# A hybrid SSD and attention block: the scan's float32 products at three places of a projection run, and two steps that change places

## The chip, the cores and the metric

One core of a Trainium2 chip runs the whole block as one program. The metric is the device time of one execution in microseconds (us), the median of the runs shown. The engines are named as the profile names them: PE (matrix products), PEld (its weight loads), DVE, ACT, POOL, and SP, which issues the DMAs.

## The reference

A LayerNorm, then a mixer, then a convolutional FFN, each with a residual and a LayerNorm, on x of 512 tokens by 1024 channels in float32. The mixer has two branches, an SSD (Mamba-2) scan and a sparse attention, projected, gated and summed. The change is in the SSD branch alone:

```python
xbc = jax.nn.silu(_causal_dwconv(xbc, conv_w, conv_b))
xs, Bm, Cm = jnp.split(xbc, [SSD_INNER, SSD_INNER + SSD_GROUPS * SSD_STATE], axis=-1)
...
y = _ssd_scan(xs * dt[..., None], dt * A, Bm, Cm)
y = (y + xs * D_skip[:, None]).reshape(Bsz, L, SSD_INNER)
v = (y * jax.nn.silu(z)).astype(jnp.float32).reshape(Bsz, L, SSD_GROUPS, SSD_INNER // SSD_GROUPS)
v = v * lax.rsqrt(jnp.mean(v * v, -1, keepdims=True) + LN_EPS)
return (v.reshape(Bsz, L, SSD_INNER) * norm_g).astype(z.dtype)
```

The scan goes chunk by chunk: products of C and B under a decay mask, times X, for what lies inside a chunk; states of B and X carried from chunk to chunk, times C, for the rest. There are 4 groups of 4 channel tiles (128 channels each, two heads of 64).

## The kernel before

Channels lie on the partitions and 512 tokens on the free axis. A projection is eight steps; a step is three fp32r products of 128 by 128 weights with 512 tokens (weights and activations are split into a high and a low part, `whi`/`wlo` by ACT and DVE from each loaded tile `wraw`). `in_x`, `in_b`, `in_c` project a tile of X, B or C and end in `conv_silu` (two ACT instructions, four DVE instructions out of the PSUM bank `acc`); `in_z` projects a gate; `out_br(g, s)` projects group g's normalized scan result, two halves of four steps each.

The scan's own products are plain float32. For each channel tile j of group g there are: `ssd_x` (four transposes into a `tr` bank, DVE makes `xdd` and `xd` of them, SP loads the decay tile `G` and `eaB`); `ssd_s` (states: three products into bank a or b, then a chain of four DVE instructions makes `pv`); `ssd_g` and `ssd_gm` (ACT and DVE turn `G` into the masked decay); `ssd_y` (three products of `pv` with C, into a or b, DVE multiplies them into `eaB`); and `ssd_d`, for two tiles at once (eight half-width products for each tile, into banks c and a, then `v` on DVE and POOL). Each float32 product stands in the trace as two instructions, except for transposes. Besides, for each group there are `ssd_b` (four transposes of B), `ssd_cb` (C times B and the mask `cbm`), `ssd_root` (sums of squares, a square root on DVE and POOL) and `ssd_norm` (its broadcast by four transposes, then `v` to `yhi`, `ylo`).

The order of the work is written by hand. `run(projs, items)` goes through the steps of a list of projections and issues, after step k, what `items` holds for k. `pair(g, j, at, ...)` makes the items of channel tiles j and j+1. While `chain[0]` is true, each PE instruction is made to follow the one issued before it, so PE's order is the program's. The other engines' order is made by the scheduler of the tile framework, before the kernel runs; each engine takes its list in that order. There are nine runs of the scan: a first one without `pair`, then one for each two channel tiles. PSUM has eight banks: three `acc`, two `tr`, and a, b, c. After the runs come attention, the output projection and the FFN; the top-k selection for attention (`select`, L582 to L586) stands on DVE between scan work.

Of the kernel before, what the change touches and what calls it, by code (L numbers as in the profile page):

```python
# [57 lines left out]
def tok(i):  # L58
    return slice(i * P, (i + 1) * P)
# [6 lines left out]
def half_of(h):  # L66
    return slice(h * T, (h + 1) * T)
# [3 lines left out]
def block_kernel(ctx, tc, A, out):  # L71
# [16 lines left out]
    def wt(tag, shape, name, dtype=F32):  # L88
        return wk.tile(shape, dtype, name=name, tag=tag, bufs=BUFS[tag])
# [12 lines left out]
    def st(shape, name):  # L102
        return sml.tile(shape, F32, name=name, tag=name)

    def ps(tag, bufs=1):
        return ps_.tile([P, T], F32, name="p" + tag, tag=tag, bufs=bufs)

    def acc_tile():
        return ps("acc", 3)

    def tr_tile():
        return ps("tr", 2)
# [15 lines left out]
    for i in range(NT):  # L128
        t = wt("k4" if i < 2 else "g4", [P, D], "x")
# [35 lines left out]
    def rsqrt_small(src, scale, eps, n, i=0):  # L165

        v = st([P, n], f"rs_v{n}_{i}")
        nc.vector.tensor_scalar(v, src, scale, eps, OP.mult, OP.add)
        y = st([P, n], f"rs_y{n}_{i}")
        last_pow[0] = nc.gpsimd.tensor_tensor(y, v, mhalf[:, :n], OP.pow)  # L170
        return y
# [31 lines left out]
    def w_(name, s, **kw):  # L203
        return wload(A[name][s], **kw)
# [9 lines left out]
    def mm(p, a, b, start, stop):  # L214
        pe(nc.tensor.matmul(p, a, b, start=start, stop=stop).ins)  # L215
# [35 lines left out]

    def rms_root(sqs, n):

        s4 = ps("b")
        for i in range(NT):
            for j, sq in enumerate(sqs):
                mm(s4[:, i:i + 1], sq[:, tok(i)], ones[:, 0:1], start=j == 0, stop=j == len(sqs) - 1)
        return rsqrt_small(s4[:, :NT], 1.0 / n, EPS, NT)
# [8 lines left out]
    def steps(p, w, rhs, off=0):  # L267
        for k in range(len(rhs)):
            proj(p, w, rhs, off=off, part=(k, k + 1))
            if k < len(rhs) - 1:  # L270
                yield
# [46 lines left out]
    for i, t in enumerate(xt):  # L318
# [5 lines left out]
        v, y, nm = st([P, 1], f"x_v{i}"), st([P, 1], f"x_y{i}"), st([P, 1], f"x_nm{i}")  # L324
# [270 lines left out]
    def conv_silu(dst, p, c):  # L595

        y = wt("cv", [P, T], "cv")
        nc.scalar.activation(y, p, AF.Identity, bias=cwb[:, 96 + c:97 + c], scale=cwb[:, 72 + c:73 + c])
        for k in (2, 1, 0):
            d = 3 - k  # L600
            nc.vector.scalar_tensor_tensor(y[:, d:], p[:, :T - d], cwb[:, 24 * k + c:24 * k + c + 1],  # L601
                                           y[:, d:], OP.mult, OP.add)
        nc.scalar.activation(dst, y, AF.Tanh)
        nc.vector.scalar_tensor_tensor(dst, dst, 1.0, y, OP.add, OP.mult)


    def in_b(g):

        bc = wt("k4", [P, 2, T], "bc")
        sins[g] = {"BT": bc[:, 0], "CT": bc[:, 1], "xs": [], "core": [], "v": []}  # L610
        p = acc_tile()
        yield from steps(p, w_("w_xbc", 16 + g), hT)
        conv_silu(bc[:, 0], p, 16 + g)
        yield

    def in_c(g):

        p = acc_tile()
        yield from steps(p, w_("w_xbc", 20 + g), hT)
        conv_silu(sins[g]["CT"], p, 20 + g)  # L620
        yield

    def in_x(g, j):

        p = acc_tile()
        yield from steps(p, w_("w_xbc", 4 * g + j), hT)
        xj = wt("xs", [P, T], "xs")
        conv_silu(xj, p, 4 * g + j)
        sins[g]["xs"].append(xj)
        yield  # L630

    def in_z(g, j):

        p = acc_tile()
        yield from steps(p, w_("w_z", 4 * g + j), hT)
        zs = wt("m2", [P, T], "zs")
        nc.scalar.activation(zs, p, AF.Tanh, scale=0.5)
        nc.vector.scalar_tensor_tensor(zs, zs, 1.0, p, OP.add, OP.mult)
        sins[g]["z", j] = zs
        ssd_gate(g, j)  # L640
        yield

    def out_br(g, s):

        w = w_("w_br_ssd", 4 * g + s)
        for j in range(2):
            n = 2 * s + j
            p = acc_tile()
            yield from steps(p, w, sins[g]["y"], off=T * j)
            if g == 0:  # L650
                nc.scalar.activation(mssd[:, n], p, AF.Copy)
            else:
                nc.vector.tensor_tensor(mssd[:, n], mssd[:, n], p, OP.add)
            yield
# [94 lines left out]
    def ssd_d(g, js):  # L749

        s_ = sins[g]
        yds = [ps(t) for t in "ca"]
        for j, yd in zip(js, yds):
            xd, xdd, G, eaB, pv = s_["core", j]
            for c in range(NT):
                for h in range(2):
                    mm(yd[h * 64:(h + 1) * 64, tok(c)], xd[:, c, h], G[:, h, c], start=True, stop=True)
        for j, yd in zip(js, yds):
            q = 4 * g + j
            eaB = s_["core", j][3]  # L760
            v = wt("v", [P, T], "v")
            last_v[0] = nc.vector.scalar_tensor_tensor(v, s_["xs"][j], Dv[:, q:q + 1], yd, OP.mult, OP.add)  # L762
            nc.gpsimd.tensor_tensor(v[:, P:], v[:, P:], eaB[:, P:], OP.add)  # L763
            s_["v"].append(v)
            ssd_gate(g, j)

    def ssd_gate(g, j):

        s_ = sins[g]
        if len(s_["v"]) <= j or ("z", j) not in s_:  # L770
            return
        v = s_["v"][j]
        nc.gpsimd.tensor_tensor(v, v, s_["z", j], OP.mult)
        if "ssum" not in s_:
            s_["ssum"] = wt("m2", [P, T], "ssum")
            nc.scalar.activation(s_["ssum"], v, AF.Square)
        else:
            sq = wt("m2", [P, T], "sq")
            nc.scalar.activation(sq, v, AF.Square)
            nc.gpsimd.tensor_tensor(s_["ssum"], s_["ssum"], sq, OP.add)  # L780

    AT = (2, 6, 13, 18, 28, 32, 40)

    def ssd_root(g):
        sins[g]["r"] = rms_root([sins[g]["ssum"]], 4 * T)
# [49 lines left out]
    def run(projs, items):  # L835

        k = 0
        for p in projs:
            for _ in p:
                for f, *args in items.get(k, ()):  # L840
                    f(*args)
                k += 1
        assert k > max(items), (k, items)

    def pair(g, j, at, more=(), root=11, norm=20):

        items = {}
        more = [*more]
        if g and not j:
            more += [(root, ssd_root, g - 1), (norm, ssd_norm, g - 1)]  # L850
        x0, x1, s0, s1, y0, y1, d = at
        for n in range(4):
            more += [(s0 + 1 + n, ssd_g, g, j, n), (s1 + 1 + n, ssd_g, g, j + 1, n)]
        more += [(x0, ssd_x, g, j), (x1, ssd_x, g, j + 1), (s0, ssd_s, g, j, "a"), (s1, ssd_s, g, j + 1, "b"),
                 (s1 + 4, ssd_gm, g, j), (s1 + 7, ssd_gm, g, j + 1),
                 (y0, ssd_y, g, j, "a"), (y1, ssd_y, g, j + 1, "b"), (d, ssd_d, g, (j, j + 1))]
        for k, *f in more:
            items.setdefault(k, []).append(f)
        return items

    def scored(*ks):
        return [(k, next, score, None) for k in ks]

    def pin():
# [5 lines left out]
    first_items[44] = [(ssd_cb, 0)]  # L870
    run([in_b(0), in_c(0), out_ga(0), in_x(0, 0), out_ga(1), in_x(0, 1)], first_items)
    run([in_x(0, 2), in_z(0, 0), in_x(0, 3), in_z(0, 1), in_b(1)],
        pair(0, 0, (2, 12, 15, 21, 28, 31, 37), scored(*range(1, 40, 3))))
    run([in_x(1, 0), in_x(1, 1), in_z(0, 2), in_c(1), in_z(0, 3), in_x(1, 2)],
        pair(0, 2, AT, [*scored(3, 5, 7), (21, ssd_b, 1)]))
    for g in (1, 2):
        run([in_x(g, 3), in_b(g + 1), in_z(g, 0), in_z(g, 1), out_br(g - 1, 0), out_br(g - 1, 1), in_c(g + 1)],
            pair(g, 0, AT, [(1, ssd_cb, 1), (18, t5_load), (46, t5_rows)] if g == 1 else ()))
        run([in_x(g + 1, 0), in_z(g, 2), out_br(g - 1, 2), in_x(g + 1, 1), in_z(g, 3), out_br(g - 1, 3),
             in_x(g + 1, 2)], pair(g, 2, AT, [(11, ssd_b, g + 1), (21, ssd_cb, g + 1), (42, pin)]))  # L880
    run([in_x(3, 3), in_z(3, 0), in_z(3, 1), in_z(3, 2), out_br(2, 0)],
        pair(3, 0, (0, 4, 11, 16, 25, 28, 36), [(37, pin)]))
    run([out_br(2, 1), in_z(3, 3), out_br(2, 2), out_br(2, 3)],
        pair(3, 2, (0, 3, 9, 13, 21, 23, 30)))
    chain[0] = False


# [201 lines left out]
    for i in range(NT):  # L1089
        for j in range(2):  # L1090
            t = h1[i][:, half_of(j)]
# [36 lines left out]
    for k in range(KR, KW):  # L1128
        d = [wop.tile([P, D], F32R, name=f"wo{k}{j}", tag=f"wo{k}{j}") for j in range(2)]
# [7 lines left out]
    for i in range(NT):  # L1137
# [6 lines left out]
        for j in range(2):  # L1144
            t = h1[i][:, half_of(j)]
# [221 lines left out]
```

## Time and profile before

| | |
|---|---|
| median of 3 runs | 1104.15 us (1103.95 to 1104.29) |
| profiled execution, its own time | 1103.91 us |
| its span, first to last instruction | 1102.2 us |
| mean granted TensorE clock | 0.998 |
| PE busy | 1089.3 us (99% of the span) |
| DVE, ACT, POOL busy | 772.5, 479.0, 167.3 us |

The 1.7 us between the span and the execution's time lie around the instructions. Matmuls are pipelined, so a busy PE is not a PE at its peak: how far apart matmuls start says more than how long one lasts.

### The profile page before, as it was taken

The numbers are of one execution on the slowest core, as the hardware profiler recorded it, in microseconds if no ns is written. First come the engines' busy times: TensorE is split into PE (matmuls) and PEld (weight loads), VectorE is DVE, ScalarE is ACT, GpSimd is POOL, SyncE is SP. The second block draws the span as 40 slices with busy tenths as digits, with TensorE's granted clock in tenths as the row PEclk, the third lists the DMA queues.
The fourth block names the chain that finished last, engine by engine and source line by source line (L and its number), as shares of the span: only waits on it lengthen the run. The fifth ranks groups of instructions, "written<-read, shape, count | busy, mean of one in ns | idle before, by whom it ended". The sixth has DMA issues, their size and how long they took to land.

```text
span 1102.2 us, 14649 instructions
## 1 busy us (share of the span) xinstructions
PE 1089.3 (99%) x5452; PEld 901.2 (82%) x5452; DVE 772.5 (70%) x1403; ACT 479.0 (43%) x825; POOL 167.3 (15%) x183
## 2 busy tenths in 40 slices
PE   8999999999999999999999999999999999999997
PEld 7888888788788888888787878888888888888885
DVE  7667887579967999668999958466656666542227
ACT  6345565453553643355555525115444444431220
POOL 3000203202112023023333460130000000000002
PEclk9999999999999999999999999999999999999999
DMA  7442324454244242322222356403333232322232
GB/s 285 144 150 86 117 77 136 160 177 144 87 131 134 77 134 96 120 93 74 78 72 89 125 175 203 150 1 96 98 99 98 102 99 96 97 96 95 96 96 77
DMA packets 41783, 125.71 MB, mean 114 GB/s; under 512 B 4736, under 2 KB 9392, under 8 KB 41712
## 3 DMA queue, kind: packets, MB, share of 16 engines
q1 hardware_dynamic: 41712, 124.77, 34.9%
q8 instruction: 43, 0.70, 0.3%
q14 instruction: 28, 0.23, 0.1%
HBM read 118.31 MB, written 9.59 MB: 116 GB/s over the span
## 4 chain that ended last, share of the span: by engine, by line
PE 90%; DVE 7%; issue 1%; DMA 1%; ACT 1%; POOL 0%; DVEq 0%
PE pacc L215 54%; PE pc L215 6%; PE pacc L239 6%; PE pb L215 5%; PE pa L215 4%; PE ptr L239 4%; PE ptr L215 3%; PE pb L239 2%; PE pc L239 2%; PE pa L239 2%; DVE mask L585 1%; DVE wlo L189 1%; PE pa L218 1%; DVE m L584 1%; PE ptr L218 1%
## 5 line engine op out<-in xcount | busy, mean ns | idle before, releaser
L189 DVE TENSOR_TENSOR wlo<-wraw,whi 128x1024 fp32r<-128x1024 f32 x159 | 202.1, 1271 | 184.1 <-ACT whi L188 183.6
L188 ACT ACTIVATE whi<-wraw 128x1024 fp32r<-128x1024 f32 x159 | 168.2, 1058 | 237.6 <-PE pacc L215 155.6
L215 PE MATMUL pacc<-hhi,whi 128*128 128x512 f32 (+1 forms) x536 | 219.4, 409 | 0.8 <-ACT hhi L378 0.8
L215 PE MATMUL pacc<-hlo,whi 128*128 128x512 f32 (+1 forms) x536 | 210.5, 393 | 0.8 <-DVE hlo L381 0.8
L215 PE MATMUL pacc<-hhi,wlo 128*128 128x512 f32 (+1 forms) x536 | 209.0, 392 | 0.4 <-DVE wlo L189 0.3
L215 PEld LDWEIGHTS pacc<-hlo,whi 128*128 128x128 f32 (+1 forms) x536 | 100.5, 187 | 24.7 <-DVE hlo L381 2.3
L215 PEld LDWEIGHTS pacc<-hhi,whi 128*128 128x128 f32 (+1 forms) x536 | 100.9, 188 | 19.4 <-issue 1.5
L215 PEld LDWEIGHTS pacc<-hhi,wlo 128*128 128x128 f32 (+1 forms) x536 | 100.9, 188 | 18.2 <-DVE wlo L189 0.7
L215 PE MATMUL pacc<-h1hi,wlo 128*128 128x512 f32 (+1 forms) x216 | 79.0, 366 | 0.0
L215 PE MATMUL pacc<-h1hi,whi 128*128 128x512 f32 (+1 forms) x216 | 78.9, 366 | 0.0
L215 PE MATMUL pacc<-h1lo,whi 128*128 128x512 f32 (+1 forms) x216 | 78.7, 366 | 0.0
L964 POOL TENSOR_TENSOR tm<-mask,toe 128x128 f32<-128x128 f32 (+1 forms) x64 | 44.5, 699 | 159.5 <-DVE mn L975 97.2
L1251 POOL TENSOR_TENSOR rs_y<-rs_v,mhalf 128x1 f32<-128x1 f32 x4 | 4.0, 1002 | 353.8 <-DVE rs_v L1250 349.2
L601 DVE SCALAR_TENSOR_TENSOR cv<-pacc,cwb,cv 128x511 f32<-128x511 f32 (+2 forms) x72 | 53.3, 741 | 0.5
L215 PE MATMUL pacc<-ylo,whi 128*128 128x512 f32 x128 | 50.3, 393 | 1.3 <-DVE ylo L175 1.3
L215 PE MATMUL pacc<-yhi,whi 128*128 128x512 f32 x128 | 51.6, 404 | 0.0
L215 PE MATMUL pacc<-yhi,wlo 128*128 128x512 f32 x128 | 49.9, 390 | 0.0
L763 POOL TENSOR_TENSOR v<-v,eaB 128x384 f32<-128x384 f32 x16 | 17.0, 1079 | 210.2 <-DVE v L762 147.9
L978 ACT ACTIVATE l<-l,mn 128x128 f32<-128x128 f32 (+1 forms) x64 | 35.7, 558 | 30.3 <-DVE mn L975 28.9
L215 PEld LDWEIGHTS pacc<-h1hi,whi 128*128 128x128 f32 x216 | 40.8, 189 | 6.7
L215 PEld LDWEIGHTS pacc<-h1hi,wlo 128*128 128x128 f32 x216 | 40.8, 189 | 6.5
L215 PEld LDWEIGHTS pacc<-h1lo,whi 128*128 128x128 f32 x216 | 40.5, 188 | 6.5
(481 smaller groups left out, 2268.7 us busy)
## 6 DMA issues: line engine op xcount, KB each, us to landing
wraw<-in_w_up_dram SPq DMA_DIRECT2D x44, 512.0 KB, 3.5
wraw<-in_w_xbc_dram SPq DMA_DIRECT2D x24, 512.0 KB, 3.5
wraw<-in_w_down_dram SPq DMA_DIRECT2D x22, 512.0 KB, 3.5
G<-ac_d SPq DMA_DIRECT2D x16, 512.0 KB, 5.6
wraw<-in_w_z_dram SPq DMA_DIRECT2D x16, 512.0 KB, 3.5
wraw<-in_w_br_ssd_dram SPq DMA_DIRECT2D x16, 512.0 KB, 3.5
wraw<-in_w_ga_dram SPq DMA_DIRECT2D x8, 512.0 KB, 3.5
eaB<-ea_d SPq DMA_DIRECT2D x32, 128.0 KB, 5.5
```

Of the source, the lines that this page charges most:

```text
L188: nc.scalar.activation(hi[:, :cols], raw[:, :cols], AF.Copy)
L189: nc.vector.tensor_tensor(lo[:, :cols], raw[:, :cols], hi[:, :cols].bitcast(F32), OP.subtract)
L215: pe(nc.tensor.matmul(p, a, b, start=start, stop=stop).ins)
L218: pe(nc.tensor.transpose(p, a, b).ins)
L239: nc.tensor.matmul(p, x[a][:, tok(i)], w[b][h], start=first and j == 0, stop=last and j == 2)
L584: nc.vector.max(out=m8, in_=S)
L585: nc.vector.match_replace(out=S, in_to_replace=m8, in_values=S, imm_value=-3.4e38)
L601: nc.vector.scalar_tensor_tensor(y[:, d:], p[:, :T - d], cwb[:, 24 * k + c:24 * k + c + 1], y[:, d:], OP.mult, OP.add)
L763: nc.gpsimd.tensor_tensor(v[:, P:], v[:, P:], eaB[:, P:], OP.add)
L964: nc.gpsimd.tensor_tensor(tm[:, :K - f], maskt[i][:, f:], self.toe[:, 2 * P - K + f:], OP.add)
L978: nc.scalar.activation(l[:, :K], l[:, :K], AF.Exp, bias=self.mn[:, ic], scale=-1.0, accum_out=self.sm[:, ic])
L1251: nc.gpsimd.tensor_tensor(y, v, mhalf[:, :1], OP.pow)
```

## The change

`pair` takes three places in place of seven: x (both `ssd_x`), s (both `ssd_s`, behind `ssd_root` of the group before where there is one) and y (both `ssd_y` and then `ssd_d`). `ssd_root` takes bank c in place of b, and `ssd_d` takes c and a `tr` tile in place of c and a. `ssd_cb` and `ssd_b` stand where a pair's products stand already. In groups 1 and 2, `in_c(g + 1)` goes from the end of the first run into the second, and `out_br(g - 1, 2)` from the second run to the end of the first. The masked decay of the first run of groups 1 and 2 (`gm`) is issued at 26 and 29.

```diff
     def rms_root(sqs, n):
-        s4 = ps("b")
+        s4 = ps("c")
...
     def ssd_d(g, js):
         s_ = sins[g]
-        yds = [ps(t) for t in "ca"]
+        yds = [ps("c"), tr_tile()]
...
-    AT = (2, 6, 13, 18, 28, 32, 40)
+    AT = (3, 12, 38)
...
-    def pair(g, j, at, more=(), root=11, norm=20):
-
-        items = {}
-        more = [*more]
+    def pair(g, j, at, more=(), norm=None, gm=None):
+
+        x, s0, y = at
+        gm = gm or (s0 + 7, s0 + 11)
+        items = {x: [(ssd_x, g, j), (ssd_x, g, j + 1)],
+                 s0: [(ssd_s, g, j, "a"), (ssd_s, g, j + 1, "b")],
+                 y: [(ssd_y, g, j, "a"), (ssd_y, g, j + 1, "b"), (ssd_d, g, (j, j + 1))]}
         if g and not j:
-            more += [(root, ssd_root, g - 1), (norm, ssd_norm, g - 1)]
-        x0, x1, s0, s1, y0, y1, d = at
+            items[s0].insert(0, (ssd_root, g - 1))
+            more = [*more, (norm or s0 + 7, ssd_norm, g - 1)]
         for n in range(4):
-            more += [(s0 + 1 + n, ssd_g, g, j, n), (s1 + 1 + n, ssd_g, g, j + 1, n)]
-        more += [(x0, ssd_x, g, j), (x1, ssd_x, g, j + 1), (s0, ssd_s, g, j, "a"), (s1, ssd_s, g, j + 1, "b"),
-                 (s1 + 4, ssd_gm, g, j), (s1 + 7, ssd_gm, g, j + 1),
-                 (y0, ssd_y, g, j, "a"), (y1, ssd_y, g, j + 1, "b"), (d, ssd_d, g, (j, j + 1))]
-        for k, *f in more:
+            more = [*more, (s0 + 1 + n, ssd_g, g, j, n), (s0 + 6 + n, ssd_g, g, j + 1, n)]
+        for k, *f in [*more, (gm[0], ssd_gm, g, j), (gm[1], ssd_gm, g, j + 1)]:
             items.setdefault(k, []).append(f)
         return items
...
     run([in_x(0, 2), in_z(0, 0), in_x(0, 3), in_z(0, 1), in_b(1)],
-        pair(0, 0, (2, 12, 15, 21, 28, 31, 37), scored(*range(1, 40, 3))))
+        pair(0, 0, (10, 18, 36), scored(1, 4, 7, 14, 16, 20, 22, 24, 26, 28, 30, 32, 34)))
     run([in_x(1, 0), in_x(1, 1), in_z(0, 2), in_c(1), in_z(0, 3), in_x(1, 2)],
-        pair(0, 2, AT, [*scored(3, 5, 7), (21, ssd_b, 1)]))
+        pair(0, 2, AT, [*scored(0, 8, 10), (38, ssd_b, 1)]))
     for g in (1, 2):
-        run([in_x(g, 3), in_b(g + 1), in_z(g, 0), in_z(g, 1), out_br(g - 1, 0), out_br(g - 1, 1), in_c(g + 1)],
-            pair(g, 0, AT, [(1, ssd_cb, 1), (18, t5_load), (46, t5_rows)] if g == 1 else ()))
-        run([in_x(g + 1, 0), in_z(g, 2), out_br(g - 1, 2), in_x(g + 1, 1), in_z(g, 3), out_br(g - 1, 3),
-             in_x(g + 1, 2)], pair(g, 2, AT, [(11, ssd_b, g + 1), (21, ssd_cb, g + 1), (42, pin)]))
+        run([in_x(g, 3), in_b(g + 1), in_z(g, 0), in_z(g, 1), out_br(g - 1, 0), out_br(g - 1, 1), out_br(g - 1, 2)],
+            pair(g, 0, AT, gm=(26, 29), more=[(12, ssd_cb, 1), (18, t5_load), (46, t5_rows)] if g == 1 else ()))
+        run([in_x(g + 1, 0), in_z(g, 2), in_c(g + 1), in_x(g + 1, 1), in_z(g, 3), out_br(g - 1, 3),
+             in_x(g + 1, 2)], pair(g, 2, AT, [(12, ssd_b, g + 1), (38, ssd_cb, g + 1), (42, pin)]))
     run([in_x(3, 3), in_z(3, 0), in_z(3, 1), in_z(3, 2), out_br(2, 0)],
-        pair(3, 0, (0, 4, 11, 16, 25, 28, 36), [(37, pin)]))
+        pair(3, 0, (1, 10, 34), [(37, pin)]))
     run([out_br(2, 1), in_z(3, 3), out_br(2, 2), out_br(2, 3)],
-        pair(3, 2, (0, 3, 9, 13, 21, 23, 30)))
+        pair(3, 2, (1, 9, 29)))
```

## Rows read from the trace of the kernel before

**Rows 1.** The page: the chain that ended last, by engine.

```profile
PE 90%; DVE 7%; issue 1%; DMA 1%; ACT 1%; POOL 0%; DVEq 0%
```

**Rows 2.** Windows over the scan, 93 to 418 us: their sum, busy us by engine.

```profile
sum 325.00, PE 323.58 PEld 268.12 DVE 264.82 ACT 166.50 POOL 54.31; mean PE 40.45 PEld 33.51 DVE 33.10 ACT 20.81 POOL 6.79
```

**Rows 3.** The chain in order of time, an FFN projection: start, us, what.

```profile
768.16 5.44 PE pc L215 x24
```

**Rows 4.** PE's groups by shape, 93 to 418 us: count | busy, mean ns.

```profile
L215 PE MATMUL pa<-xdd,bt 128*128 128x128 f32 x48 | 6.7, 276 | 0.0
```

**Rows 5.** Timeline of PE, group 2: transposes, root and states (start us, us).

```profile
268.43 0.39 PE L215 MATMUL pacc<-hlo,whi 128*128 128x512 f32 x1
268.66 0.60 PE L218 MATMUL ptr<-ident,xs 128*128 128x128 f32 x4
...
272.33 0.39 PE L215 MATMUL pacc<-hlo,whi 128*128 128x512 f32 x1
272.56 0.95 PE L215 MATMUL pb<-ones,ssum 128*128 128x1 f32 x8
...
274.62 0.39 PE L215 MATMUL pacc<-hlo,whi 128*128 128x512 f32 x1
274.85 0.83 PE L215 MATMUL pa<-xdd,bt 128*128 128x128 f32 x6
...
278.73 0.39 PE L215 MATMUL pacc<-hlo,whi 128*128 128x512 f32 x1
```

**Rows 6.** Timeline of PE, group 3: root and states at one place.

```profile
365.10 0.39 PE L215 MATMUL pacc<-hlo,whi 128*128 128x512 f32 x1
365.33 0.95 PE L215 MATMUL pb<-ones,ssum 128*128 128x1 f32 x8
366.14 0.92 PE L215 MATMUL pa<-xdd,bt 128*128 128x128 f32 x6
...
370.11 0.39 PE L215 MATMUL pacc<-hlo,whi 128*128 128x512 f32 x1
```

**Rows 7.** Timeline of PE around one `ssd_d`.

```profile
204.42 0.39 PE L215 MATMUL pacc<-ylo,whi 128*128 128x512 f32 x1
204.74 1.09 PE L215 MATMUL pc<-G,xd 128*64 128x128 f32 x16
...
206.64 0.50 PE L215 MATMUL pacc<-yhi,whi 128*128 128x512 f32 x1
```

**Rows 8.** Waits of PE, 93 to 418 us: total, times, longest.

```profile
PE pacc L215 <- DVE ylo L175: 1.3, 2, 1.1
```

**Rows 9.** Timelines of DVE and PE at the longer of these waits.

```profile
291.41 1.21 DVE L720 TENSOR_TENSOR G<-G,cbm 128x1024 f32<-128x1024 f32 x1
...
293.20 1.28 DVE L175 TENSOR_TENSOR ylo<-v,yhi 128x512 fp32r<-128x512 f32 x2
...
293.94 0.50 PE L215 MATMUL pacc<-ylo,whi 128*128 128x512 f32 x1 [1.10 <-DVE ylo L175]
```

**Rows 10.** Timeline of POOL: the square root of group 1's `ssd_root`.

```profile
274.97 1.01 POOL L170 TENSOR_TENSOR rs_y<-rs_v,mhalf 128x4 f32<-128x4 f32 x1 [12.72 <-DVE rs_v L168]
```

**Rows 11.** The page, DMA issues: count, KB each, us to landing.

```profile
G<-ac_d SPq DMA_DIRECT2D x16, 512.0 KB, 5.6
```

**Rows 12.** Timelines of ACT, DVE and PE: group 0's second X tile.

```profile
98.00 1.06 ACT L188 ACTIVATE whi<-wraw 128x1024 fp32r<-128x1024 f32 x1 [1.57 <-PE pacc L215]
...
99.63 0.62 ACT L603 ACTIVATE xs<-cv 128x512 f32<-128x512 f32 x1
...
100.90 0.68 DVE L604 SCALAR_TENSOR_TENSOR xs<-xs,cv 128x512 f32<-128x512 f32 x1
...
101.94 0.60 PE L218 MATMUL ptr<-ident,xs 128*128 128x128 f32 x4
```

**Rows 13.** Timelines of PE and DVE: transposes of the last pair, their evictions.

```profile
391.58 0.60 PE L218 MATMUL ptr<-ident,xs 128*128 128x128 f32 x4
...
394.06 0.68 DVE L703 TENSOR_TENSOR xd<-ptr,dt 128x512 f32<-128x512 f32 x1
```

## The prediction

> **What bounds the kernel now.** I read four views. First the chain of work that ended last: 90% of it is PE and 7% DVE [rows 1], so a change gains what it takes off PE's time line, and loses what PE then waits for. Second the windows over the scan, the only part that the change touches: in 325 us PE is busy 323.6, DVE 264.8 (81%), ACT 166.5 [rows 2]. A busy PE hides small losses, so the third view is the timeline of PE, read by the distance from one start to the next. The undisturbed distance is that of an FFN projection, where 24 fp32r products take 5.44 us [rows 3]: 0.2267 us for a product, 0.68 us for a step of three. What lies above that in the scan is what can be won. Fourth are PE's waits in the scan: a single kind, for `ylo`, twice, 1.3 us in all [rows 8]. So little is to be won, and the work is to find what can be lost.
>
> **A switch between float32 and fp32r.** The number of places at which PE goes over to float32 products and back follows from the lists of items. Before: seven for each of 8 pairs, 56; one `ssd_b` for group 1; in group 1's two runs `ssd_cb`, `ssd_root`, `ssd_norm`, `t5_rows`, `ssd_b`, `ssd_cb`; in group 2's four of these; in group 3's `ssd_norm`. That is 68. After: three for each pair, 24, three `ssd_norm` and `t5_rows`, 28. So 40 switches go; no product does.
>
> What is one worth? In the timeline of group 2 [rows 5] the fp32r product ahead of the transposes starts at 268.43 and the fifteenth behind them at 272.33. Of these 3.90 us, 15 x 0.2267 = 3.40 are fp32r, so the four transposes cost 0.50. They stand (0.60 - 0.28) / 3 = 0.11 apart (one lasts 0.28, [rows 4]), 0.44 for four: 0.06 is left for the switch. The six state instructions take 278.73 - 274.62 - 3.40 = 0.71 and stand (0.83 - 0.28) / 5 = 0.11 apart, 0.66: 0.05 is left. A merged place exists: in group 3 root and states share one [rows 6], and 370.11 - 365.10 - 3.40 = 1.61 us. Apart, in group 2, the root takes 274.62 - 272.33 - 6 x 0.2267 = 0.93, and with the 0.71 that is 1.64. Merging saved 0.03, though only six products stand behind that root to show its whole price. I take 0.05, with bounds 0.03 and 0.06: 40 x 0.05 = **2.0 us gained** (1.2 to 2.4). The switch shows as a loss in the rows; the Trainium skill's TensorE: Matmul & The Clock Gate, Part 2, has PE pull weight loads ahead of running products, by which a switch should cost nothing, and by that rule this term is 0 (a rival below).
>
> **`ssd_d` behind `ssd_y`.** Its half-width products start 0.32 us after the last fp32r product, 0.09 more than the usual 0.23 [rows 7]. Behind a full-width float32 product no `ssd_d` stands in the trace. If the array needs no pause there, the 0.09 goes, 8 x 0.09 = 0.7 us gained; if the 0.32 stays, counted from the start of a product that takes 0.11, the loss beyond its pitch is 0.21, 0.12 more than before, 8 x 0.12 = 1.0 us lost. I take 0, between the two: a float32 instruction occupies 0.11 where the fp32r one occupies 0.23, so a pause measured from the end of either would be alike. The row shows a pause at the entry; the Trainium skill's TensorEngine Tiling (Array Packing), Key Properties, says why: changing the tiling mode "drains the TensorE". By this rule eight changes in and eight out stay, whatever stands ahead of them.
>
> **The waits for `ylo`.** In group 2's first run `out_br` reaches a product for which `ylo` is not ready: PE starts at 293.94, after 1.10 us of waiting. DVE did the masked decay (`ssd_gm`, 1.21 us from 291.41) ahead of the two `ylo` it needed [rows 9]. Afterwards these two instructions are issued at 26 and 29, behind `ssd_norm` at 19, which itself comes a step earlier (20 before), and the `pv` chains are done from step 12 on. That takes 2.4 us of DVE from ahead of `ylo`, more than the 1.1 that was missing. So **1.3 us gained**, with bounds 0 (DVE's order is the scheduler's and may keep the old one) and 1.3. Next late there would be the eviction of an `out_br` half, with three `acc` banks for cover: two more halves, 8 steps, 5.4 us.
>
> **The two moved steps.** `in_c` brings its 24 products, a weight load on SP, its split on ACT and DVE, two more ACT and four more DVE instructions; `out_br` its 24 products, load, split and two evictions. They trade slots, so SP still passes one 512 KB weight load for each projection, in the same queue behind the same neighbours. DVE gets the conv later; `ssd_cb` needs C at 38, and `in_c` ends at 23: 15 steps, 10.2 us, cover it. Cost 0; bound, if C is late, what DVE is behind by, 3.2 us in the worst row below. `ssd_x`'s loads on SP move too: `G` takes 5.6 us to land [rows 11], and from x to the first `ssd_g` there are 10 steps (9 in the last pair), 6.8 (6.1) us. If one came later, ACT would stand at it with the weight splits behind; the buffer is freed two steps earlier than before (`ssd_d` at 38 for 40), which is the cover. Cost 0.
>
> **Bank and root.** `ssd_norm` follows `ssd_root` by seven steps, nine before. Its square root ended at 275.98 [rows 10], some 2.6 us behind the root's last products, and seven steps are 4.8 us. Bank c and the second `tr` bank have been read many steps before their next use. Cost 0.
>
> **The first pair.** Its transposes of the second X tile ran at 101.94; the tile was ready at 100.90 + 0.68 = 101.58 [rows 12], 0.4 us early. They now come at step 10 for 12: two steps (1.36) and a score (two short products, some 0.35) earlier, about 100.2. Ready as before, the tile would hold PE for 1.4 us. But its tanh on ACT (99.63) waited behind a weight split that itself stood 1.57 us for PE, and DVE loses two evictions (1.2 us) from ahead of the conv. If the conv ends before 98.0 the tanh fits into that gap. Bounds 0 and 1.4; I take 0.2, since the gap is longer than the tanh. **0.2 us lost.**
>
> **The sum.** 2.0 + 1.3 - 0.2 = 3.1 us. The profiled execution took 1103.91 us (span 1102.2, 1.7 around it), so 1100.8; the median of the runs is 0.24 above that execution, so the forecast is 1101.0. A change of 0.2%, 2.2 us, is about what can be told from none: below 1101.9 is faster, above 1106.4 slower.
>
> **The rivals.**
> 1. DVE keeps the waits for `ylo`. For: DVE is at 81%, and its order is decided before the run. Against: `ssd_gm` now follows in program order. 1101.0 + 1.3 = 1102.3. Chance 0.15.
> 2. A switch costs nothing once the places are merged, so the change doesn't do what it says: the merged row saved just 0.03. 1101.0 + 2.0 = 1103.0. Chance 0.09.
> 3. `ssd_d`'s entry pays 0.32 behind float32 too: 1101.0 + 1.0 = 1102.0. Chance 0.10.
> 4. The second X tile holds PE in the first pair for the whole 1.4: 1101.0 + 1.2 = 1102.2. Chance 0.10.
> 5. Slower: DVE is late with `xdd`. Both tiles' transposes come at once, and both states products nine steps later (8 in two pairs), 6.1 us, for 11 and 12 steps before. In the last pair the eviction of one tile ended at 394.74, 3.2 us after its transposes began [rows 13]; with the second tile's pair behind it (1.2) that is 4.4 us, 1.7 short of 6.1. So it takes DVE another 1.7 us behind to cost anything, and 2.4 at each of eight places to cost 5.6 us: 1106.6. For: the bursts (two `eaB`, two `v`, two pairs of evictions) are twice as long. Against: PE asks for no eviction during a long float32 place. Chance 0.12, with what else makes PE wait often.
>
> The forecast itself has 0.44, with a range of its own from 1099.8 (2.4 + 1.3 + 0.7 gained off 1103.91, and the median's 0.24) to 1102.0 (1.2 + 1.3 gained, 0.4 of new waits lost).
>
> **The numbers.** The range must leave out two in ten: 1099.2 to 1105.0 takes in everything but the slower case and a little of each end; below 1099.8 only waits smaller than those that the profile names could go. Faster: 0.40 of the forecast's 0.44, half of rivals 3 and 4 (0.10), a little of 1 and 2 (0.05): 0.55. Slower: 0.12 and 0.02 from the others: 0.14. No change that can be told: 0.31.
>
> **What would show it.** In the new profile each pair has three float32 places, root and states as one of 1.6 us; the start of the scan to its end is some 3 us shorter, all later stages shifted alike. PE's waits in the scan lose the row for `ylo`. The first product of `ssd_d` shows its distance to the last `ssd_y` product: 0.11, 0.2 or 0.32. PE's waits for `xdd`, `xs`, `G` or a `tr` bank would show the rivals. I am wrong if such waits add up to over 2 us, or if DVE's order in the second runs, which now hold four convs, makes PE wait for an `acc` bank.

## The result, and the profile after

The changed kernel takes 1109.64 us, the median of 6 runs (1108.36 to 1110.97); the kernel before took 1104.09 beside it. The ratio is 1.0051, with a 95% interval from 1.0038 to 1.0064: slower by 5.5 us, where 3 us of gain were forecast. The profiled execution is the longest of the six, 1110.97 us with a span of 1109.2, 7.06 us above that of before.

The views of [rows 1], [rows 2] and [rows 8] come first: the chain by engine; windows over the scan with two of the stretches (us, busy us and count by engine, granted clock, DMA share, GB/s); PE's waits in the scan (total, times, longest).

```profile
PE 94%; DVE 3%; ACT 2%; issue 0%; DMA 0%; POOL 0%; DVEq 0%
```

```profile
165.00:207.00 42.00, 39.77 (x193) 33.20 (x192) 30.18 (x46) 22.59 (x43) 8.66 (x7) 0.96 0.39 114
...
253.00:300.00 47.00, 43.91 (x229) 36.68 (x229) 45.11 (x98) 23.32 (x44) 10.01 (x8) 0.95 0.37 103
...
sum 325.00, PE 319.18 PEld 267.19 DVE 260.56 ACT 165.44 POOL 55.99; mean PE 53.20 PEld 44.53 DVE 43.43 ACT 27.57 POOL 9.33
```

```profile
PE pacc L215 <- DVE zs L638: 5.3, 2, 3.1
PE ptr L215 <- ACT rel L512: 0.4, 1, 0.4
```

The chain looks better than before, 94% PE for 90%, which says nothing of the time. The windows say where to look: PE stands idle for 42 - 39.77 = 2.2 us and 47 - 43.91 = 3.1 us in two stretches, the first runs of groups 1 and 2, where the clock too is below 1. The waits name the cause: not `ylo` any more, but `zs`, the last DVE instruction of a gate (`in_z`). The timeline of PE in group 1 and a window behind the wait show the price:

```profile
197.17 0.39 PE L215 MATMUL pacc<-hlo,whi 128*128 128x512 f32 x1
199.79 0.78 PE L215 MATMUL pacc<-yhi,whi 128*128 128x512 f32 x1 [2.23 <-DVE zs L638]
200.37 0.63 PE L215 MATMUL pacc<-yhi,wlo 128*128 128x512 f32 x1
200.79 0.63 PE L215 MATMUL pacc<-ylo,whi 128*128 128x512 f32 x1
...
203.55 0.40 PE L215 MATMUL pacc<-yhi,whi 128*128 128x512 f32 x1
```

```profile
200.00:203.00 3.00, 3.00 (x8) 2.32 (x9) 3.00 (x5) 0.00 (x0) 0.00 (x0) 0.50 0.64 175
```

`out_br`'s first product starts 2.62 us behind the product ahead of it, 2.39 beyond its pitch. Behind the wait the products stand up to 0.43 us apart and the granted clock is 0.50, the lower of its two levels (1.2 GHz): to 203.55 nine products take 3.76 us for 2.04, another 1.7. The same places in group 2:

```profile
292.60 0.39 PE L215 MATMUL pacc<-hlo,whi 128*128 128x512 f32 x1
296.07 0.80 PE L215 MATMUL pacc<-yhi,whi 128*128 128x512 f32 x1 [3.09 <-DVE zs L638]
...
302.46 0.40 PE L215 MATMUL pacc<-yhi,whi 128*128 128x512 f32 x1
```

The wait costs 3.24 us beyond the pitch, and the 15 products up to 302.46 another 6.39 - 3.40 = 3.0. That is 10.3 us at two places.

The rest goes into the 7.06 as follows. In the first pair PE waited for a score's relu (`rel`) and lost 0.8 at two products (0.24 and 0.58 beyond the pitch); the two old waits [rows 8] are gone, 1.65 by their pitches. That makes 10.3 + 0.8 - 1.65 = 9.45, so some 2.4 us were gained elsewhere. The merged places gave 2.0 to 2.25 of them by medians (shown below); the small rest was not followed, and executions of the kernel before alone differ by 0.4.

**Why a bank is late.** Group 1 shows it best: PE gets to `out_br` at the same time as before (the product ahead starts at 197.17, 197.08 before). ACT's timeline after and, in the second fence, before:

```profile
182.80 2.14 ACT L712 ACTIVATE G<-G,acT 128x128 f32<-128x128 f32 x7
...
185.83 2.44 ACT L712 ACTIVATE G<-G,acT 128x128 f32<-128x128 f32 x8
...
190.07 0.77 ACT L598 ACTIVATE cv<-pacc,cwb 128x512 f32<-128x512 f32 x1
```

```profile
183.49 2.44 ACT L712 ACTIVATE G<-G,acT 128x128 f32<-128x128 f32 x8
...
186.78 0.77 ACT L598 ACTIVATE cv<-pacc,cwb 128x512 f32<-128x512 f32 x1
...
188.55 2.45 ACT L712 ACTIVATE G<-G,acT 128x128 f32<-128x128 f32 x8
```

Each tile's decay passes (`ssd_g`) are tied behind that tile's copy of `pv`, and so behind its states. With both states at one place ACT does both tiles' passes in one stretch, and the first pass of `in_b`'s convolution (L598), which stood between them, starts 3.3 us later, at 190.07. DVE's list, after and before:

```profile
189.41 2.72 DVE L795 SCALAR_TENSOR_TENSOR v<-v,ngh,pc 128x512 f32<-128x512 f32 x4 [2.45 <-PE pc L218]
...
194.32 0.74 DVE L601 SCALAR_TENSOR_TENSOR cv<-pacc,cwb,cv 128x511 f32<-128x511 f32 x1
194.98 1.21 DVE L720 TENSOR_TENSOR G<-G,cbm 128x1024 f32<-128x1024 f32 x1
196.11 1.89 DVE L175 TENSOR_TENSOR ylo<-v,yhi 128x512 fp32r<-128x512 f32 x3
...
199.05 0.68 DVE L638 SCALAR_TENSOR_TENSOR zs<-zs,pacc 128x512 f32<-128x512 f32 x1
199.65 0.74 DVE L601 SCALAR_TENSOR_TENSOR cv<-pacc,cwb,cv 128x510 f32<-128x510 f32 x1
```

```profile
186.92 1.22 DVE L189 TENSOR_TENSOR wlo<-wraw,whi 128x1024 fp32r<-128x1024 f32 x1 [2.43 <-ACT whi L188]
188.06 0.74 DVE L601 SCALAR_TENSOR_TENSOR cv<-pacc,cwb,cv 128x511 f32<-128x511 f32 x1
...
193.91 0.73 DVE L601 SCALAR_TENSOR_TENSOR cv<-pacc,cwb,cv 128x509 f32<-128x509 f32 x1
```

Before, DVE did the convolution's first pass at 188.06 and its third at 193.91, and a bank was free. Now it stands idle for 2.45 us just then; the convolution begins at 194.32, behind `v`, a mask and a weight split, and at 199.65 it is in its second pass. The idle time is not the difference, since DVE stood idle for 2.43 us before too; what came behind it is. ACT explains 3.3 of the 6.3 us by which DVE's first pass comes later. The rest is the order of DVE's list, which has `v`, the mask and the split first, though ACT's pass had ended at 190.84. All three `acc` banks are held, one by the convolution and two by gates, and `out_br` gets the one that `zs` frees.

### The profile page after: what moved, and what is told of

It is laid out like the page before. It is cut to its first block, busy times and chain, and to the rows that moved or that the text cites. A ratio compares the mean times of both kernels' runs of the same rounds, so it can differ in the third digit from the quotient of the medians.

```text
span 1109.2 us, 14634 instructions
## 1 busy us (share of the span) xinstructions
PE 1091.3 (98%) x5452; PEld 905.7 (82%) x5452; DVE 774.6 (70%) x1403; ACT 477.8 (43%) x825; POOL 169.5 (15%) x183
## 4 chain that ended last, share of the span: by engine, by line
PE 94%; DVE 3%; ACT 2%; issue 0%; DMA 0%; POOL 0%; DVEq 0%
PE pacc L215 57%; PE pc L215 7%; PE pacc L239 6%; PE pb L215 5%; PE pa L215 4%; PE ptr L239 4%; PE ptr L215 3%; PE pb L239 2%; PE pc L239 2%; PE pa L239 2%; ACT G L712 1%; PE pa L218 1%; PE ptr L218 1%; PE pb L218 1%; DVE wlo L189 0%
## 5 line engine op out<-in xcount | busy, mean ns | idle before, releaser
L215 PE MATMUL pacc<-hhi,whi 128*128 128x512 f32 (+1 forms) x536 | 216.1, 403 | 0.8 <-ACT hhi L378 0.8
```

## The experiments

Three theories were set against each other. T1: the merged states make ACT's burst of decay, and the convolution behind it holds up DVE and the banks (the 5.7 us of its expectations is group 2's figure, in which PE's own loss in group 1 is contained; group 1 shows 3.3). T2: what counts is DVE's two masks ahead of `zs`. T3: the two projections that change places load DVE here. Later came T4: in group 2's first run DVE itself is the engine without slack. Times are medians; the ratio is to the kernel before, run beside each (1104.02 to 1104.22); the last column is PE's waits in the scan by that view (total, times, longest; "none" where it lists none).

| kernel | us | ratio, 95% interval | PE waits for |
|---|---|---|---|
| changed | 1109.64 | 1.0051 [1.0038, 1.0064] | zs 5.3, 2, 3.1; rel 0.4, 1, 0.4 |
| 1 states apart | 1103.60 | 0.9996 [0.9987, 1.0004] | zs 2.3, 1, 2.3; ylo 0.3, 1, 0.3 |
| 2 projections back | 1110.61 | 1.0061 [1.0048, 1.0073] | zs 5.3, 2, 3.1; rel 0.4, 1, 0.4; mssd 0.4, 1, 0.4 |
| 3 masks behind zs | 1105.28 | 1.0010 [1.0001, 1.0019] | zs 1.4, 2, 0.8; ylo 0.8, 1, 0.8; rel 0.4, 1, 0.4; cv 0.2, 1, 0.2 |
| 4 decay held | 1102.82 | 0.9986 [0.9977, 0.9995] | zs 1.4, 1, 1.4; rel 0.4, 1, 0.4 |
| 5 idle filled | 1106.90 | 1.0026 [1.0015, 1.0036] | rel 0.4, 1, 0.4; zs 0.2, 1, 0.2 |
| 6 states alone merged | 1109.21 | 1.0042 [1.0029, 1.0054] | zs 4.9, 3, 2.2 |
| 7 = 1, rounds moved | 1101.30 | 0.9977 [0.9968, 0.9986] | cv 0.8, 1, 0.8; ylo 0.3, 1, 0.3 |
| 8 = 4, rounds moved | 1100.70 | 0.9970 [0.9959, 0.9982] | rel 0.4, 1, 0.4 |
| 9 before, rounds moved | 1102.74 | 0.9986 [0.9978, 0.9995] | ylo 0.5, 2, 0.2 |
| 10 changed, rounds moved | 1109.10 | 1.0042 [1.0029, 1.0054] | zs 5.1, 2, 2.9; rel 0.4, 1, 0.4 |
| 11 = 8, first pair apart | 1099.89 | 0.9961 [0.9948, 0.9975] | none |
| 12 transposes spread | 1105.83 | 1.0014 [1.0006, 1.0023] | pv 1.1, 1, 1.1; rel 0.5, 1, 0.5; ylo 0.2, 1, 0.2 |

**1. The second tile's states apart again.**

```diff
-                 s0: [(ssd_s, g, j, "a"), (ssd_s, g, j + 1, "b")],
+                 s0: [(ssd_s, g, j, "a")], s0 + 5: [(ssd_s, g, j + 1, "b")],
```

> One edit to the changed kernel: the states of a pair's second tile (ssd_s) stand five steps behind the first tile's, as they stood before the change; everything else stays merged. Theory T1 (both state places at one point let ACT do both tiles' decay in one stretch, in_b's convolution comes 5.7 us later, DVE's work piles up ahead of zs, and out_br waits for an acc bank): out_br's two waits, 2.2 and 3.1 us after the change, fall to 1 us or less each, the granted clock stays at its upper level behind them, and the time is 1101 to 1104 us, some 6 to 8 below the changed kernel's 1109.6. Eight more switches at 0.05 us give back 0.4 us of that. Theory T2 (the two masks issued together on DVE ahead of zs, whatever ACT does): here the masks' items stay at their steps, so the waits stay at 2 us or more, 1108 to 1110. Theory T3 (the two projections that change places): the waits stay, 1109 to 1110.

The one edit took back 6 us, to a time that can't be told from that of before. Group 1's wait is gone altogether, as T1 says and T2 and T3 don't; in group 2 a wait of 2.3 us is left, which T1 did not expect. Its timeline of PE:

```profile
287.65 0.39 PE L215 MATMUL pacc<-hlo,whi 128*128 128x512 f32 x1
290.34 0.50 PE L215 MATMUL pacc<-yhi,whi 128*128 128x512 f32 x1 [2.30 <-DVE zs L638]
290.67 0.39 PE L215 MATMUL pacc<-yhi,wlo 128*128 128x512 f32 x1
290.90 0.40 PE L215 MATMUL pacc<-ylo,whi 128*128 128x512 f32 x1
```

Behind this wait the products stand 0.23 us apart: the clock did not fall in this execution.

**2. The two projections back at their old places.**

```diff
-        run([in_x(g, 3), ..., out_br(g - 1, 1), out_br(g - 1, 2)],
+        run([in_x(g, 3), ..., out_br(g - 1, 1), in_c(g + 1)],
-        run([in_x(g + 1, 0), in_z(g, 2), in_c(g + 1), ...
+        run([in_x(g + 1, 0), in_z(g, 2), out_br(g - 1, 2), ...
```

> The changed kernel with in_c(g + 1) and out_br(g - 1, 2) back at their old places; the three merged places stay. T1 and T2: what stands ahead of out_br's first product is the same, both waits stay within 0.5 us of 2.2 and 3.1 us, and the time is 1108.5 to 1110.5 us. T3 (the exchange of the two projections loads DVE at this place): both waits go, 1100 to 1103 us.

The same two waits to a tenth, and one of 0.4 us more: T3 falls. The median is 1.0 us above the changed kernel's, 0.1 beyond the expected range, with executions from 1109.56 to 1112.45: no gain or loss by the exchange of the steps can be told.

**3. The masks behind the gate on DVE.** In the first run of groups 1 and 2 both `ssd_gm` are ordered behind `zs`.

```diff
+        if g in (1, 2) and j < 2:
+            tc.add_manual_dep(i.ins, sins[g]["zi", 0].name, NOSYNC, reason="order")
```

> The changed kernel, with DVE's two masks (ssd_gm, 2.4 us together) of the first run of groups 1 and 2 put behind zs, the gate's last DVE instruction; nothing else moves, ACT's burst of decay stays. T2 (the two masks make zs late): zs ends 2.4 us earlier, the waits of 2.2 and 3.1 us fall to 0 and 0.7 us, no lower clock behind them, so all 10.3 us that the two places lose come back: 1099 to 1102 us. T1 in its strict form (what is late is in_b's convolution, behind ACT's burst): zs still waits for its place behind the convolution's own DVE work, some 1 to 1.5 us of each wait stays: 1102 to 1106 us. If the masks are then late for ssd_y, PE waits there for G and this is seen as a row of its own.

`zs`'s waits fell to 0.6 and 0.8 us, between what the two theories said, and 1.0 us of new waits came behind them, for `ylo` and for the convolution (`cv`). The masks are a part of the queue ahead of `zs`; with them out of it DVE is late with the next thing. The time, 1105.28 us, lies in T1's range. ACT's burst stayed (the convolution's first pass on ACT at 189.90), and yet 4.4 us came back: the burst does its harm mostly through what stands ahead of `zs` in DVE's list.

**4. The second tile's decay held on ACT.** All products stay at the merged places; in the first run of groups 1 and 2 the second tile's decay passes come behind the convolution's first pass in ACT's list.

```diff
+            if g in (1, 2) and j == 1:
+                tc.add_manual_dep(i.ins, last_conv[0].ins.name, NOSYNC, reason="order")
```

> The changed kernel, with the second tile's four decay passes on ACT (8 instructions, some 2.5 us) of the first run of groups 1 and 2 held behind the first ACT pass of in_b's convolution; all products on PE stay at their places. T1 (ACT's burst delays in_b's convolution): the convolution's first pass starts 2.5 us earlier or more, DVE does it ahead of the masks, both waits of out_br fall to 1 us or less, the clock stays up, 1100 to 1104 us. T2 (the masks): the waits stay above 1.5 us in both groups, 1106 to 1110 us.

ACT's and DVE's timelines in group 1 (lines two to four higher than those of after):

```profile
183.29 2.15 ACT L714 ACTIVATE G<-G,acT 128x128 f32<-128x128 f32 x7
...
188.22 0.77 ACT L600 ACTIVATE cv<-pacc,cwb 128x512 f32<-128x512 f32 x1
188.88 2.44 ACT L714 ACTIVATE G<-G,acT 128x128 f32<-128x128 f32 x8
```

```profile
189.68 0.74 DVE L603 SCALAR_TENSOR_TENSOR cv<-pacc,cwb,cv 128x511 f32<-128x511 f32 x1
...
195.97 0.74 DVE L603 SCALAR_TENSOR_TENSOR cv<-pacc,cwb,cv 128x509 f32<-128x509 f32 x1
```

The convolution stands between the two tiles' passes again, 1.85 us earlier than in after (less than the 2.5 expected); DVE starts it 4.6 us earlier and is through with its third pass before 197, and `out_br` waits no more in group 1. So 6.8 us come back with not one product moved on PE, and with both masks still ahead of `zs` in DVE's list (187.40 and 194.23): the states' place on PE was not the cost, but what it released on ACT and, behind that, the order of DVE's list. Group 2 keeps 1.4 us, more than T1 said.

**5. The idle time filled.** Products that nothing reads stand ahead of the two waits.

```diff
+    def fill(n):
+        p = tr_tile()
+        for i in range(n):
+            mm(p, hT[0][0][:, :P], hT[1][0], start=i == 0, stop=i == n - 1)
...
+            more=[(31, fill, 9), ...] if g == 1 else [(31, fill, 13)]
```

> The changed kernel with products that nothing reads put into the two idle stretches: ahead of out_br's first product in the first run of group 1 nine fp32r products of 128x512 (9 x 0.227 = 2.0 us), in that of group 2 thirteen (2.9 us), into a tr bank. DVE's and ACT's lists stay, so zs comes as late as before and the wait itself stays paid (what is left of idle is 0.2 us at each place); only the idleness goes. If the lower clock behind the two waits comes from the idleness, the products behind them stay at 0.227 us a piece, and the time falls by what the lower clock cost, 1.8 and 3.4 us in the profiled execution and by the granted clock of the others somewhat less: 1104 to 1107 us, and a narrower spread of the executions. If the lower clock is something else (the products of out_br themselves, or the time of day), the pitches of 0.427 us stay and the time is 1109 to 1111.

(By the pitches shown above, the lower clock cost 1.7 and 3.0 us, not 1.8 and 3.4.)

```profile
291.25 3.11 PE L215 MATMUL ptr<-hhi 128*128 128x512 f32 x13
294.49 0.50 PE L215 MATMUL pacc<-yhi,whi 128*128 128x512 f32 x1
294.83 0.39 PE L215 MATMUL pacc<-yhi,wlo 128*128 128x512 f32 x1
295.06 0.40 PE L215 MATMUL pacc<-ylo,whi 128*128 128x512 f32 x1
```

`out_br` comes 3.24 us behind the first filling product, as late as its wait made it, and behind it the pitch is 0.23. The time falls by 2.7 us, and eight runs lie within 0.5 us (1106.76 to 1107.23) where the changed kernel's six spread over 2.6. So half of the 5.5 us lost is the clock, which falls here because PE stands idle.

**6. Only the states merged, in the kernel before,** in the first run of groups 1 and 2 alone.

```diff
-(s1, ssd_s, g, j + 1, "b"),
+(s0 if g in (1, 2) and not j else s1, ssd_s, g, j + 1, "b"),
```

> The kernel before, with one edit: in the first run of groups 1 and 2 the states of the second tile stand beside the first tile's, five steps earlier; all other places, steps and masks are those of before. T1 (this merge alone makes ACT's burst of decay): in_b's convolution on ACT starts 4 us or more later in both runs, out_br or what stands behind it waits for an acc bank 1.5 to 3.5 us in each, and the time is 1106 to 1111 us. Rival (the burst does harm only together with the other merged places or the masks' steps): at most one wait of over 1 us, 1103 to 1105.

Six products moved by five steps, in two of the runs, cost 5 us: T1. The convolution's first pass came 2.75 us later in group 1 (189.53 on ACT, for 186.78 before), less than the 4 us expected, and 4.7 us later in group 2 (284.40 for 279.70); the waits came in both, 2.25 us in group 1, 1.66 and 0.96 in group 2. The masks stand at their old steps here, so T2 is not needed for the waits.

**7 to 10. The top-k rounds.** Experiments 1 and 4 left a wait in group 2 alone, where DVE also works at the top-k rounds of the first attention mask (`select`), tied by `pin` to group 1's last result. The edit ties them to group 2's first run.

```diff
-             ...] if g == 1 else ()))
+             ...] if g == 1 else [(42, pin)]))
...
-             ..., (38, ssd_cb, g + 1), (42, pin)]))
+             ..., (38, ssd_cb, g + 1), *([(42, pin)] if g == 2 else [])]))
```

On top of experiment 1: 

> The kernel with the second tile's states apart again, and besides the top-k rounds of the first mask (22 rounds of some 0.85 us on DVE between 250 and 293 us) tied to a scan result of group 2 in place of group 1, so that they start some 48 us later. Theory T4 (in group 2's first run DVE is the engine without slack, 44.4 of 47 us, and that is why 2.3 us of wait were left there): the wait goes or falls under 0.4 us, 1100 to 1102 us, faster than the kernel before. Rival (DVE is as late for lack of the convolution's ACT pass): the wait stays over 1.5 us, 1103 to 1104. If the rounds come too late for the attention stage, the time is lost there and the row of the wait is gone all the same.

On top of experiment 4: 

> The kernel with all three places merged and the second tile's decay held behind in_b's convolution on ACT, and besides the first mask's top-k rounds moved out of group 2's first run as in the run beside it. T4: the wait of 1.4 us goes, 1100.5 to 1102 us, the fastest or the second fastest here. Rival: it stays, 1102.5 to 1103.

In the kernel before: 

> The kernel before, with the one edit that moves the first mask's top-k rounds out of group 2's first run. The wait of 1.10 us for ylo at 293.94 stands in that run, where DVE had 46.2 of 47 us; it should go, the one of 0.23 us in group 1 stay, and the later stages be unchanged: 1102.6 to 1103.4 us. If this edit alone gave most of what the kernel with held decay and moved rounds gains (1100.7), so 1101.5 or less, then the merged places would be worth next to nothing; by the switch at 0.03 to 0.05 us the merged places are worth 1.2 to 2 us of the 3.3.

In the changed kernel: 

> The changed kernel with the one edit that moves the first mask's top-k rounds out of group 2's first run; ACT's burst of decay stays. T1: group 1 has no top-k rounds, so its wait of 2.2 us stays; in group 2 DVE has slack, but the convolution's ACT pass still comes late, so a wait of 1.0 to 2.4 us is left of the 3.1; 1105.5 to 1108.5 us. Rival (DVE without slack is the whole cause in group 2): the wait there falls under 0.5 us, 1104 to 1105.5.

The window of group 2's first run, of experiment 4 and, in the second fence, of 8:

```profile
253.00:300.00 47.00, 45.55 (x244) 37.61 (x243) 44.80 (x97) 23.68 (x44) 7.93 (x8) 1.00 0.34 106
```

```profile
253.00:300.00 47.00, 46.96 (x252) 39.28 (x251) 35.86 (x56) 24.52 (x46) 8.90 (x8) 1.00 0.35 115
```

DVE goes from 44.8 to 35.9 us and PE's last wait in the run with it: T4 holds, though experiment 7 keeps 0.8 us where under 0.4 was expected. In the kernel before the same edit takes 1.45 us off, within the forecast, so moving the rounds accounts for less than half of the 3.3 us that experiment 8 gains. In the changed kernel it gives 0.5 us, less than the spread of either kernel (1107.19 to 1110.43 with the edit), and the wait stays 2.9; DVE there even stands idle for ACT:

```profile
280.25 0.69 DVE L604 SCALAR_TENSOR_TENSOR xs<-xs,cv 128x512 f32<-128x512 f32 x1 [1.71 <-ACT xs L603]
```

More slack on DVE does not help while the burst on ACT stands: the wait was more than the 1.0 to 2.4 us expected and the time, 1109.10, above its range, which speaks for T1 and against DVE's load as the whole cause. The two bind one after the other.

**11. The states of the first pair apart, on top of 8.**

```diff
-                 s0: [(ssd_s, g, j, "a"), (ssd_s, g, j + 1, "b")],
+                 s0: [(ssd_s, g, j, "a")],
...
+        items[s0 if g or j else s0 + 5] = items.get(s0 if g or j else s0 + 5, []) + [(ssd_s, g, j + 1, "b")]
```

> The fastest kernel so far (three merged places, the second tile's decay held on ACT in groups 1 and 2, the first mask's rounds moved), and in the first pair the second tile's states five steps behind the first's. In the first pair the burst of decay on ACT stood ahead of the scores' relu, two waits of PE, 0.24 and 0.59 us beyond the pitch; apart they should go, for one or two switches at 0.05: 1099.9 to 1100.4 us.

The two waits for a score's relu go, and 0.8 us with them: the same burst on ACT, in another run. This version beats both kernels, by 4.3 us and 9.75.

**12. The transposes spread.** Each `ssd_x` puts one transpose behind each of four steps.

```diff
             mm_t(tr[:, c], x_[:, tok(c)], ident)
+            if c < NT - 1 and (g or j > 1):
+                yield
```

> The kernel before, with the four transposes of a channel tile put one behind each of four steps in place of all behind one (seven of the eight pairs): 41 more places at which PE goes over to float32 and back, and not one product more. If a switch costs 0.05 us, 2.0 us lost: 1105.8 to 1106.6 us; at 0.026 (what the first product behind a place shows) 1.1 us: 1105.0 to 1105.5; if a switch costs nothing, 1104.0 to 1104.5. In the trace the first fp32r product behind a single transpose starts later than the pitch by the price.

```profile
221.36 0.40 PE L215 MATMUL pacc<-hlo,whi 128*128 128x512 f32 x1
221.60 0.27 PE L218 MATMUL ptr<-ident,xs 128*128 128x128 f32 x1
221.63 0.48 PE L215 MATMUL pacc<-hhi,whi 128*128 128x512 f32 x1
...
222.40 0.27 PE L218 MATMUL ptr<-ident,xs 128*128 128x128 f32 x1
```

The time alone would fit 0.04 us a switch, but new waits for `pv` (1.1) and a relu (0.5) are in it, and the old wait of 1.10 is out, so it can't be read as the price. The rows can: a step with one transpose takes 222.40 - 221.60 = 0.80 us, 0.12 over 0.68, of which the transpose is 0.11; 43 such steps in this trace take 0.81 on average. With three products between switches, one costs some 0.01 to 0.02 us.

## Why the prediction was wrong

**The switches: right.** The timeline of PE after, in group 2, answers to [rows 5]: both tiles' transposes, then root and both states at one place.

```profile
269.94 0.39 PE L215 MATMUL pacc<-hlo,whi 128*128 128x512 f32 x1
270.17 1.03 PE L218 MATMUL ptr<-ident,xs 128*128 128x128 f32 x8
...
274.24 0.39 PE L215 MATMUL pacc<-hlo,whi 128*128 128x512 f32 x1
...
276.96 0.39 PE L215 MATMUL pacc<-hlo,whi 128*128 128x512 f32 x1
277.19 0.95 PE L215 MATMUL pc<-ones,ssum 128*128 128x1 f32 x8
278.00 0.91 PE L215 MATMUL pa<-xdd,bt 128*128 128x128 f32 x6
278.75 0.83 PE L215 MATMUL pb<-xdd,bt 128*128 128x128 f32 x6
...
282.61 0.39 PE L215 MATMUL pacc<-hlo,whi 128*128 128x512 f32 x1
```

By the same sum as in the prediction, to the fifteenth product behind: 274.24 - 269.94 - 3.40 = 0.90 for eight transposes, for 2 x 0.50 apart, 0.10 for one switch; and 282.61 - 276.96 - 3.40 = 2.25 for 0.93 + 0.71 + 0.71, 0.10 for two. From the kernel before with moved rounds to experiment 11 the time falls 2.85 us; its two remaining waits were worth 0.8 (two pitches of 0.62 for 0.23), and 2.05 is left for 39 switches (2.25 if the 0.20 us that one product is late in experiment 11, at 290.22, are counted), 0.05 to 0.06 each. So the 2.0 us were there, and rival 2 is wrong. What the prediction drew from the Trainium skill's TensorE: Matmul & The Clock Gate, Part 2, that with weight loads pulled ahead a switch should cost nothing, is not borne out by these rows.

**`ssd_d` behind `ssd_y`: right, at 0.** In the first run of group 1 its first product stands 0.77 us behind the start of six float32 ones 0.11 apart, so 0.22 behind the last, 0.11 beyond the pitch; 0.09 before [rows 7]. Rival 3 is wrong.

```profile
206.94 0.83 PE L215 MATMUL pb<-bc,pv 128*128 128x128 f32 x6
207.71 1.09 PE L215 MATMUL pc<-G,xd 128*64 128x128 f32 x16
```

**The waits for `ylo`: the step that failed.** The prediction held that the masks, issued at 26 and 29, would go from ahead of `ylo`, and that next late would be the eviction of an `out_br` half, "with three `acc` banks for cover". The masks did not go: in group 1 DVE still does both ahead of `ylo` (the second at 194.98, `ylo` at 196.11). The waits for `ylo` vanished because PE already stood at `out_br`'s first product, for something later. And the cover wasn't there: when `out_br` begins, its three banks are held by the convolution and two gates, none of them by an `out_br` half. The prediction asked which wait goes and which instructions move on DVE; it didn't follow ACT's list, where the decay is tied to the states that the change moves, and so costed the moved states by their products alone. The text does name the outcome, PE waiting for an `acc` bank, among what would make it wrong, but lays it to the four convs of the second runs. It came in the first runs.

**The clock: no term at all.** The sum priced a wait at its own length. Here 5.6 us of waiting beyond the pitch brought another 4.7, nearly all at the lower clock, in the profiled execution; in the median it was 2.7, by what filling the idle time gave back.

**The first pair: a size not far off, another place.** 0.2 was put down, 0.8 measured, and not for the second X tile, whose transposes ran at 100.33 without a wait [rows 12], but for the scores behind ACT's burst. Rival 4 is wrong in its mechanism.

**The moved steps, the bank and the root: right, at 0** (experiment 2 for the steps; for the bank and the root, no wait of PE for them stands in the trace). Rival 5, slower because DVE is late with `xdd`: the sign came true, but no wait for `xdd` stands in the trace. Rival 1 had the reason right, DVE's list keeping the masks ahead of `ylo`, but not the wait: none for `ylo` is left. With the burst taken apart and the rounds moved the changed places run at 1099.9 to 1101.3: the forecast's 1100.8 is about the time of the changed kernel without its new waits (1110.97 - 10.3 - 0.8 = 1099.9).

## What to carry to other kernels

When an edit moves products together, list what each of them releases on the other engines, and what stood between those two pieces of work in their lists; that, and not the products, may set the price. Ask of the first wait that you remove which wait comes one instruction ahead of it, and count who holds each buffer at that moment. On a PE with almost no idle time a wait of two or three microseconds can cost nearly twice its length (here 5.6 us became 10.3), in some executions and not in others.

## What the runs showed of the hardware that was not expected

Behind waits of 2.2 and 3.1 us the clock fell to its lower level for some 9 and 15 products, and behind one of 2.9 in experiment 10; behind one of 2.3 (experiment 1's profiled execution), two of 2.2 in group 1 (experiment 10's and experiment 6's) and one of 1.1 [rows 9] it didn't. The same kernel differs from execution to execution: experiment 1's spread from 1102.8 (mean granted clock 0.999) to 1104.99 (0.997), and with the idle time filled the spread all but goes.

A switch between float32 and fp32r has no single price: 0.05 to 0.10 us with fifteen products counted behind it, 0.01 to 0.02 with three between one switch and the next. Where in between it grows was not tried.
